# A tuned encoder block: AH preparation, restacking, load order and down-projection sums rearranged

## The chip, the cores and the metric

The kernel runs on one core of a Trainium2 chip as one program. The metric is the device time of one execution in microseconds (us); lower is better. Engines are called as the profile calls them: PE is TensorE (matmuls; PEld its weight loads), DVE is VectorE, ACT is ScalarE, POOL is GpSimd, and SP is SyncE, which here only issues DMAs. An engine runs its instructions strictly in the order in which the program lists them. An instruction that waits holds everything behind it on its engine.

## The reference, cut to what matters

One layer of a bidirectional encoder, all float32, on 1024 rows of 1024 features:

```python
h = rms_norm(x, norm_mix_pre)
z, xbc, dt_raw, u = split(h @ w_in)
y_ssd = ssd_mixer(z, xbc, dt_raw, ...)     # convolution, chunked scan in both directions, gated norm
y_s5  = s5_mixer(u, ...)                   # 64 groups of 16 channels, 64 complex states each
x = x + rms_norm(concat(y_ssd, y_s5) @ w_out, norm_mix_post)
h = rms_norm(x, norm_ffn_pre)
f = (silu(h @ w_gate) * (h @ w_up)) @ w_down          # inner width 2816
return x + rms_norm(f, norm_ffn_post)

# s5_mixer: y = Re(C h) of two linear scans (forward, backward) + d_skip * u
#           g = gelu(y);  return g * sigmoid(g @ glu_w + glu_b)
```

## The kernel before, in words

Matmuls of the large products are done as three products of high and low halves: a cast on ACT makes the high half, a subtraction on DVE the low half.

The stages follow each other in time. First come the norm, the `u` projection and the S5 input. Then the other projection blocks (`blocks`; the last eight make `z`), under which DVE runs the S5 recurrence over the states `SH` (`rec_step`, then `pair_down`). Then the S5 output, 16 batches of four groups each, written out by hand in the loop `for i in range(16)` (`tc.manual_schedule`: the engines get the instructions in the order of the code). Then the GLU, into which a scheduler weaves the SSD units; the output product; the gate and up products of the feed-forward part; the down product; and the tail that norms and stores the result.

S5 output, batch i. `y_mm` (L812 to L814) needs four things: `U`, the batch's input; `W0`, a table of taps read back from DRAM (`w0_load`, L738); `cp`, the powers of the transition (`c_open` on ACT, L697; `c_dir` on DVE, L705 to L707, six instructions a batch); and `AH`, the states of the batch turned into the layout that a matmul wants. `restack` (L802) makes AH with eight copies of 64x254 from SH; the number of them that DVE takes is KN["rsd"], 1 of 8 for b below 11, and none from 11 on; ACT takes the rest. There are two AH tiles, filled in turn, so restack(i+2) has to wait until y_mm(i) has read. The taps of batch i+4 come from `k_mm` (L724, PE) and `k_out` (L730 on ACT, L731 on POOL), are stored to `k_d` from POOL's queue, and `w0_load` reads them back from the same queue. `y_out` (L821, ACT) is the gelu; `g_store` (L825) sends it to DRAM, eight stores for two batches, most from SP's queue. `xt_load` (L683, L685, SP's queue) fetches what c_dir and k_mm start from; in the code it stands behind the stores of its iteration. Before the loop stand restack(0), w0_load(0) and the rest of the preparation.

SSD. `dt_prep` ends with a tile `rhl` (tag "X") that eight DMAs of POOL's queue store to `rr_d` and `na_d` (L894, L895). The tile `X` of the first SSD unit (L904) has the same tag, so its copies wait for these stores.

Down product. Seven products of a Strassen-Winograd scheme, in the order P1, P2, P3, P6, P5, P7, P4, each over 11 values q. One step (a product and a q) is 12 matmuls of 128x512 (L1898). Its operands are prepared by `d_op` some steps ahead: two casts on ACT (L1879) and two subtractions on DVE (L1880). The weights `wd` have four blocks, loaded from SP's queue in P1, P2 and P3. Sums of blocks, which P6, P5, P7 and P4 need, are made by `wd_sums` (L1865) on POOL, four for each q, all of them listed under P3. `half_sum` (L1929, L1933) squares a finished half row and multiplies it by the norm's weight, on POOL except for four at the end. The tail's `final` (L1951) adds the residual, which `final_load` (L1946) fetches.

Of the kernel before, what the change touches and what calls it, by code (L numbers as in the profile page):

```python
# [9 lines left out]
F32 = mybir.dt.float32  # L10
F32R = mybir.dt.float32r
# [7 lines left out]
def _ap(t, off, dims):  # L19
# [49 lines left out]
 'gsp': [],  # L69
 'rsd': 1,  # L70
 'hq': 's',
# [25 lines left out]
 'gB': 7,  # L97
 'rse': 0,
 'ge': 13,
# [33 lines left out]
def hymba_block(ctx, tc, P, out, dbg=None, upto=99):  # L133
# [653 lines left out]
    @pri("rs")  # L787
    def restack(b):

        while len(AHs) < 2:  # L790
            AH = yp.tile([128, 2, 4, 128], F32, name=f"AH{len(AHs)}")
            pool.memset(AH[:, 0, :, 0:1], 0.0)
            pool.memset(AH[:, 1, :, 127:128], 0.0)
            AHs.append(AH)
        AH, p0 = AHs[b % 2], 2 * b
        for d in range(2):
            for j in range(2):
                for comp in range(2):
                    src = SH[64 * j:64 * j + 64, d, (0 if d == 0 else 1):(127 if d == 0 else 128), comp, p0:p0 + 2]
                    dst = AH[64 * comp:64 * comp + 64, d, :, (1 if d == 0 else 0):(128 if d == 0 else 127)]  # L800
                    dst = dst.rearrange("p (q j) k -> p q j k", j=2)[:, :, j, :].rearrange("p q k -> p k q")
                    (dve.tensor_copy if 4 * d + 2 * j + comp >= 8 - KN["rsd" if b < 11 else "rse"] else act.copy)(dst, src)  # L802

    yts = {}

    def y_mm(b):
        U, W0, cp, AH = Us_[b // 2], W0s[b], cps[b], AHs[b % 2]
        c = b % 2
        t = yts[b] = ptmp()
        for g in range(4):  # L810
            o = t[:, 128 * g:128 * g + 128]
            pe.matmul(o, W0[:, 240 * g:240 * g + 128], U[:, 4 * c + g, :], start=True, stop=False)  # L812
            pe.matmul(o, cp[:, 0, g, 1:9, :].rearrange("p n h -> p (n h)"), AH[:, 0, g, :], start=False, stop=False)
            pe.matmul(o, cp[:, 1, g, 0:8, :].rearrange("p n h -> p (n h)"), AH[:, 1, g, :], start=False, stop=True)  # L814
# [14 lines left out]
    def dt_prep():  # L829
# [54 lines left out]
        for d in range(2):  # L884
            pe.matmul(t[:, 128 * d:128 * d + 128], af[:, d].rearrange("p c h -> p (c h)"), (tri_le, tri_ge)[d], start=True, stop=True)
            pe.transpose(t[:, 256 + 128 * d:384 + 128 * d], ln[:, d].rearrange("p c h -> p (c h)"), ident)
        rhl = un.tile([128, 2, 4, 128], F32R, tag="X", name="rhl")
        rh, rl = rhl[:, 0], rhl[:, 1]
        tv = t.rearrange("p (n l) -> p n l", n=4)
# [73 lines left out]
    def unit(q, ssum):  # L963
# [40 lines left out]
        for hf in range(2):  # L1004
# [55 lines left out]
            if hf == 0:  # L1060
                yield
        with hpri("u4"):
            if q % 4 == 0:
                act.activation(ssum, y, AF.Square)
            else:
                sq = io.tile([128, 1024], F32, tag="io", name="sq")
                act.activation(sq, y, AF.Square)
                pd('ss').tensor_tensor(ssum, ssum, sq, op=ADD)
            hl = un.tile([128, 2, 8, 128], F32R, tag="hl", name="hl")
            w = vec2[:, R_N + q:R_N + q + 1]  # L1070
            yv = y.rearrange("p (k l) -> p l k", l=8)
            act.activation(hl[:, 0], yv, AF.Copy, scale=w)
            dve.scalar_tensor_tensor(hl[:, 1], yv, w, hl.bitcast(F32)[:, 0], op0=MUL, op1=SUB)
            Q[KN["cq"]].dma_start(ch_d[128 * q:128 * q + 128], hl.bitcast(F32)[:, 0])
            Q[KN["cq"]].dma_start(cl_d[128 * q:128 * q + 128], hl.bitcast(F32)[:, 1])

    @pri("gn")
    def group_norm(g, ssum):
        t = ptmp()
        sv = ssum.rearrange("p (k l) -> p l k", l=8)  # L1080
        for l in range(8):
            pe.matmul(t[:, l:l + 1], sv[:, l, :], ones[:, 0:1], start=True, stop=True)
        rms_scale(t[:, 0:8], rg[:, g, :], 1.0 / 512, 1e-5)
# [254 lines left out]
    with tc.manual_schedule():  # L1338
        next(cvs)
        pair_powers()  # L1340
        for n, blk in enumerate(blocks):
# [10 lines left out]
            if 0 <= b < 4:  # L1352
# [3 lines left out]
                c_dir(b, 1)  # L1356
            if 0 < b < 4:
                k_batch(b - 1)
            if 0 <= b + 1 < 5 and n < NB - 1:
                xt_load(b + 1)  # L1360
        if KC == 4:
            xt_load(4)
        next(cvs, None)
    rst.close()
# [24 lines left out]

    with tc.manual_schedule():  # L1390
        restack(0)
        w0_load(0)
        w0_load(1)
        u_load(0)
        k_mm(3)
        k_out(3)
        xt_load(5)
        c_open(4)
# [4 lines left out]
        u_load(2)  # L1403
        restack(1)
        qs, oth = [], others()
        for i in range(16):
            y_mm(i)
            if i + 4 < 16:
# [15 lines left out]
            qs = qs[4:]  # L1424
            if i + 6 < 16:
                xt_load(i + 6)
            if i % 2:
# [420 lines left out]
    def wd_load(n, q):  # L1848
# [3 lines left out]
        elif n == "P2":  # L1852
            bl = ((2, 1, 0),)
        elif n == "P3":
            bl = ((3, 1, 1), (1, 0, 1))
        else:
            return
# [3 lines left out]
    def wd_sums(n, q):  # L1861
        w = wd[q]
        l = {"P3": ((0, 1, 0), (1, 3, 1), (3, 3, 0), (2, 2, 3))}.get(n, ())
        for o, a, b in l:
            pool.tensor_tensor(w[:, o], w[:, a], w[:, b], op=SUB)  # L1865

# [60 lines left out]
    def half_sum(l, c):  # L1927
# [3 lines left out]
        if last:  # L1931
            final_scale(l)
        (dve if last else pool).tensor_tensor(f, f, wp2[:, HF[c]], op=MUL)  # L1933

# [76 lines left out]
```

## Time and profile before

| | us |
|---|---|
| three executions | 1672.40, 1672.16, 1668.52; median 1672.16 |
| profiled execution, its own time | 1669.68 |
| its span, first to last instruction | 1667.8 |
| PE busy | 1546.0 (93%) |
| DVE busy | 1241.3 (74%) |
| ACT busy | 730.4 (44%) |
| POOL busy | 461.4 (28%) |
| TensorE clock granted, mean | 0.971 |

Busy time is an average over stages with different limits. By the profile's time slices PE is short of work in the S5 output, about 414 to 522 us, at single places of the GLU, and in the down product between 1520 and 1580 us; between 1060 and 1420 us it hardly pauses.

### The profile page before, as it was taken

The numbers are of one execution on the slowest core, as the hardware profiler recorded it, in microseconds if no ns is written. First come the engines' busy times: TensorE is split into PE (matmuls) and PEld (weight loads), VectorE is DVE, ScalarE is ACT, GpSimd is POOL, SyncE is SP. The second block draws the span as 40 slices with busy tenths as digits, with TensorE's granted clock in tenths as the row PEclk, the third lists the DMA queues.
The fourth block names the chain that finished last, engine by engine and source line by source line (L and its number), as shares of the span: only waits on it lengthen the run. The fifth ranks groups of instructions, "written<-read, shape, count | busy, mean of one in ns | idle before, by whom it ended". The sixth has DMA issues, their size and how long they took to land.

```text
span 1667.8 us, 22199 instructions
## 1 busy us (share of the span) xinstructions
PE 1546.0 (93%) x7980; PEld 1263.7 (76%) x7980; DVE 1241.3 (74%) x1910; ACT 730.4 (44%) x1238; POOL 461.4 (28%) x455
## 2 busy tenths in 40 slices
PE   7999999999777889899999988999999999999897
PEld 6787788777775667778778766788888888787686
DVE  7549998888452687886666578788878887669777
ACT  6345632323887445444343476222223322344352
POOL 2110000000221120111110141555555544249412
PEclk9999999999898989999999998999999999999999
DMA  5553444433877657976588872332222221682234
GB/s 181 149 144 103 127 159 152 133 109 105 207 173 204 189 176 245 289 227 219 189 262 269 291 237 95 122 107 96 95 101 101 95 101 51 242 313 74 92 119 170
DMA packets 250000, 271.58 MB, mean 163 GB/s; under 512 B 29387, under 2 KB 190659, under 8 KB 249891
## 3 DMA queue, kind: packets, MB, share of 16 engines
q1 hardware_dynamic: 224515, 215.96, 41.6%
q0 software_dynamic: 12896, 33.83, 6.4%
q10 hardware_dynamic: 12480, 20.39, 3.4%
q8 instruction: 63, 1.03, 0.3%
q14 instruction: 46, 0.38, 0.1%
HBM read 185.23 MB, written 84.84 MB: 162 GB/s over the span
## 4 chain that ended last, share of the span: by engine, by line
PE 40%; DVE 10%; DMA 8%; issue 4%; ACT 4%; POOL 3%; SPq 0%; DVEq 0%; POOLq 0%; ACTq 0%
PE acc L1592 13%; PE ptmp L1592 10%; PE ptmp L1898 4%; PE acc L1169 3%; PE acc L1898 3%; DVE dop L1880 2%; PE acc L277 2%; DMA m<-m_d 2%; PE ptmp L988 1%; POOL wd L1865 1%; PE ptmp L1054 1%; DMA m_d<-m 1%; DMA oraw<-in_w_out_dram 1%; DVE cacc L756 1%; PE ptmp L1040 1%
## 5 line engine op out<-in xcount | busy, mean ns | idle before, releaser
L1169 PE MATMUL acc<-ohi,cat 128*128 128x512 f32 x512 | 173.3, 404 | 10.8 <-DMA cat<-ch_d 5.7
L277 PE MATMUL acc<-hTh,whi 128*128 128x512 f32 (+1 forms) x456 | 179.5, 394 | 0.4 <-ACT hTh L334 0.4
L277 PE MATMUL acc<-hTl,whi 128*128 128x512 f32 (+1 forms) x456 | 178.7, 392 | 0.5 <-DVE hTl L337 0.5
L277 PE MATMUL acc<-hTh,wlo 128*128 128x512 f32 (+1 forms) x456 | 178.0, 391 | 0.0
L1575 DVE TENSOR_TENSOR wop<-rawp,wop 128x512 fp32r<-128x512 f32 x120 | 137.7, 1148 | 17.9 <-ACT wop L1574 16.7
L1592 PE MATMUL ptmp<-T,wop 128*128 128x512 f32 x528 | 127.8, 398 | 4.1 <-ACT T L1748 3.7
L1592 PE MATMUL acc<-T,wop 128*128 128x512 f32 x528 | 125.7, 393 | 1.7 <-DVE T L1751 1.6
L1898 PE MATMUL ptmp<-dop 128*128 128x512 f32 x528 | 122.0, 392 | 2.9 <-DVE dop L1880 2.9
L1592 PE MATMUL acc<-B,wop 128*128 128x512 f32 x528 | 124.6, 391 | 0.0
L1169 PEld LDWEIGHTS acc<-ohi,cat 128*128 128x128 f32 x512 | 97.7, 192 | 34.4 <-DVE mix L1720 5.4
L1592 PEld LDWEIGHTS ptmp<-T,wop 128*128 128x128 f32 x528 | 101.0, 192 | 27.3 <-ACT T L1748 3.9
L1898 PEld LDWEIGHTS ptmp<-dop 128*128 128x128 f32 x528 | 100.1, 190 | 24.2 <-DVE dop L1880 3.2
L1592 PEld LDWEIGHTS acc<-T,wop 128*128 128x128 f32 x528 | 98.8, 188 | 25.1 <-DVE T L1751 3.4
L1592 PEld LDWEIGHTS acc<-B,wop 128*128 128x128 f32 x528 | 99.0, 188 | 21.9 <-DVE B L1751 0.3
L1607 ACT ACTIVATE cg<-cg 128x512 f32<-128x512 f32 x44 | 27.8, 633 | 183.0 <-DVE cg L1605 183.0
L1574 ACT CAST wop<-rawp 128x512 fp32r<-128x512 f32 x120 | 70.2, 615 | 76.7 <-POOL rawp L1549 51.2
L1880 DVE TENSOR_TENSOR dop<-da,dop 128x512 fp32r<-128x512 f32 x77 | 75.1, 975 | 37.5 <-ACT dop L1879 37.4
L1898 PE MATMUL acc<-dop 128*128 128x512 f32 x396 | 95.6, 398 | 7.4 <-DVE dop L1880 4.7
L1169 PE MATMUL acc<-olo,cat 128*128 128x512 f32 x256 | 101.9, 398 | 0.4 <-DVE olo L1133 0.4
L277 PEld LDWEIGHTS acc<-hTh,whi 128*128 128x128 f32 x456 | 86.7, 190 | 19.4 <-issue 1.7
L277 PEld LDWEIGHTS acc<-hTl,whi 128*128 128x128 f32 x456 | 86.7, 190 | 18.4 <-DVE hTl L337 1.0
L277 PEld LDWEIGHTS acc<-hTh,wlo 128*128 128x128 f32 x456 | 86.7, 190 | 17.1 <-DVE wlo L268 0.2
(368 smaller groups left out, 3400.5 us busy)
## 6 DMA issues: line engine op xcount, KB each, us to landing
ff_d<-cg POOLq DMA_DIRECT2D x77, 256.0 KB, 2.3
da<-ff_d SPq DMA_DIRECT2D x35, 512.0 KB
raw<-in_w_in_dram SPq DMA_DIRECT2D x28, 512.0 KB
cat<-ch_d SPq DMA_DIRECT2D x48, 256.0 KB
cat<-cl_d SPq DMA_DIRECT2D x48, 256.0 KB
wd<-in_w_down_dram SPq DMA_DIRECT2D x44, 256.0 KB
rawp<-in_w_gate_dram SPq DMA_DIRECT2D x10, 1024.0 KB
rawp<-in_w_up_dram SPq DMA_DIRECT2D x10, 1024.0 KB
```

The lines of the kernel that those rows point to most:

```text
L277: pe.matmul(ps, a[:, k, :], b[:, k, sl], start=(k == 0 and n == 0), stop=(k == 7 and n == 2))
L756: (pool if ct in KN['pc'] and k in KN['pk'] else dve).scalar_tensor_tensor(a[:, d], xp[:, r], w[k], a[:, d], op0=MUL, op1=ADD)
L988: pe.matmul(t[:, 256 * s + 128 * d:256 * s + 128 * d + 128], Bt[:, c, g, :], Xw[:, d, c].rearrange("p h e -> p (h e)"), start=True, stop=True)
L1040: pe.matmul(yd[64 * hh:64 * hh + 64, 128 * j:128 * j + 128], X[:, c, 64 * hh:64 * hh + 64], Ms[hh][:, j, :], start=True, stop=True)
L1054: pe.matmul(yo[:, 128 * j:128 * j + 128], Sn[:, d, st, :], CT[:, g, 128 * c:128 * c + 128], start=True, stop=True)
L1169: pe.matmul(ps, c[:, a, k % 4, :], b[:, k % 2, :], start=(k == 0 and n == 0), stop=(k == n_ - 1 and n == 2))
L1574: act.copy(t[:, 0], src)
L1575: dve.tensor_tensor(t[:, 1], src, t.bitcast(F32)[:, 0], op=SUB)
L1592: pe.matmul(ps, a[:, ai, k, :], b[:, bi, k, :], start=(k == 0 and q == 0), stop=(k == 3 and q == 2))
L1607: act.activation(cg[:, 0], cg[:, 0], AF.Silu)
L1880: dve.tensor_tensor(t[:, k, 1], src, t.bitcast(F32)[:, k, 0], op=SUB)
L1898: pe.matmul(ps, t[:, 0, a, 128 * j:128 * j + 128], t[:, 1, b, :], start=(q == 0 and n == 0), stop=(q == NP - 1 and n == 2))
```

## The change

It has five parts.

1. **AH tiles and restacking.** Batches 0 and 1 get AH tiles of their own, in the pool `ck` under the tags "xpad" and "cacc"; batches 2 and 3 start the pair that is then used in turn. From batch 2 on, copies 1, 4 and 7 of the eight run on DVE and five on ACT, up to the last batch; batches 0 and 1 run all eight on ACT. restack(0) moves into the block loop, behind block n = NB-3 (three from the end); restack(1), w0_load(0), w0_load(1) and u_load(0) stand directly behind the last block; k_batch(3) and xt_load(5) move into the block loop.
2. **Table loads.** xt_load(i+6) stands at the head of iteration i, in front of the stores of that iteration.
3. **rhl** takes a buffer of tag "hl" in place of "X".
4. **ssum** (the SSD's gated norm) keeps its elements in another order, so that the matmul reads contiguous columns.
5. **Down.** Block (1,0,1) of wd is loaded under P2 in place of P3. The 44 sums go from POOL to DVE, one for each q under P2, two under P3, one under P6. The 12 multiplications of half_sum that POOL had go to DVE.

The removed entry of the table of settings shifts line numbers: up to line 786 a line of the kernel before is one lower in the new one.

The diff without the table of settings (there 'rsd' becomes (1, 4, 7), and 'rse' goes):

```diff
@@ -787,24 +786,25 @@
     @pri("rs")
     def restack(b):
 
-        while len(AHs) < 2:
-            AH = yp.tile([128, 2, 4, 128], F32, name=f"AH{len(AHs)}")
+        if b < 4:
+
+            AH = (ck if b < 2 else yp).tile([128, 2, 4, 128], F32, name=f"AH{b}", tag=("xpad", "cacc", "AH0", "AH1")[b])
             pool.memset(AH[:, 0, :, 0:1], 0.0)
             pool.memset(AH[:, 1, :, 127:128], 0.0)
             AHs.append(AH)
-        AH, p0 = AHs[b % 2], 2 * b
+        AH, p0 = AHs[b if b < 2 else 2 + b % 2], 2 * b
         for d in range(2):
             for j in range(2):
                 for comp in range(2):
                     src = SH[64 * j:64 * j + 64, d, (0 if d == 0 else 1):(127 if d == 0 else 128), comp, p0:p0 + 2]
                     dst = AH[64 * comp:64 * comp + 64, d, :, (1 if d == 0 else 0):(128 if d == 0 else 127)]
                     dst = dst.rearrange("p (q j) k -> p q j k", j=2)[:, :, j, :].rearrange("p q k -> p k q")
-                    (dve.tensor_copy if 4 * d + 2 * j + comp >= 8 - KN["rsd" if b < 11 else "rse"] else act.copy)(dst, src)
+                    (dve.tensor_copy if 1 < b and 4 * d + 2 * j + comp in KN["rsd"] else act.copy)(dst, src)
 
     yts = {}
 
     def y_mm(b):
-        U, W0, cp, AH = Us_[b // 2], W0s[b], cps[b], AHs[b % 2]
+        U, W0, cp, AH = Us_[b // 2], W0s[b], cps[b], AHs[b if b < 2 else 2 + b % 2]
         c = b % 2
         t = yts[b] = ptmp()
         for g in range(4):
@@ -884,8 +884,8 @@
         for d in range(2):
             pe.matmul(t[:, 128 * d:128 * d + 128], af[:, d].rearrange("p c h -> p (c h)"), (tri_le, tri_ge)[d], start=True, stop=True)
             pe.transpose(t[:, 256 + 128 * d:384 + 128 * d], ln[:, d].rearrange("p c h -> p (c h)"), ident)
-        rhl = un.tile([128, 2, 4, 128], F32R, tag="X", name="rhl")
-        rh, rl = rhl[:, 0], rhl[:, 1]
+        rhl = un.tile([128, 2, 8, 128], F32R, tag="hl", name="rhl")
+        rh, rl = rhl[:, 0, 0:4], rhl[:, 1, 0:4]
         tv = t.rearrange("p (n l) -> p n l", n=4)
         act.copy(rh, tv)
         dve.tensor_tensor(rl, tv, rh.bitcast(F32), op=SUB)
@@ -1060,15 +1060,16 @@
             if hf == 0:
                 yield
         with hpri("u4"):
+
+            yv = y.rearrange("p (k l) -> p l k", l=8)
             if q % 4 == 0:
-                act.activation(ssum, y, AF.Square)
+                act.activation(ssum.rearrange("p (l k) -> p l k", l=8), yv, AF.Square)
             else:
                 sq = io.tile([128, 1024], F32, tag="io", name="sq")
-                act.activation(sq, y, AF.Square)
+                act.activation(sq.rearrange("p (l k) -> p l k", l=8), yv, AF.Square)
                 pd('ss').tensor_tensor(ssum, ssum, sq, op=ADD)
             hl = un.tile([128, 2, 8, 128], F32R, tag="hl", name="hl")
             w = vec2[:, R_N + q:R_N + q + 1]
-            yv = y.rearrange("p (k l) -> p l k", l=8)
             act.activation(hl[:, 0], yv, AF.Copy, scale=w)
             dve.scalar_tensor_tensor(hl[:, 1], yv, w, hl.bitcast(F32)[:, 0], op0=MUL, op1=SUB)
             Q[KN["cq"]].dma_start(ch_d[128 * q:128 * q + 128], hl.bitcast(F32)[:, 0])
@@ -1077,7 +1078,7 @@
     @pri("gn")
     def group_norm(g, ssum):
         t = ptmp()
-        sv = ssum.rearrange("p (k l) -> p l k", l=8)
+        sv = ssum.rearrange("p (l k) -> p l k", l=8)
         for l in range(8):
             pe.matmul(t[:, l:l + 1], sv[:, l, :], ones[:, 0:1], start=True, stop=True)
         rms_scale(t[:, 0:8], rg[:, g, :], 1.0 / 512, 1e-5)
@@ -1354,13 +1355,17 @@
                 c_dir(b, 0)
                 run_steps(KN["r3"])
                 c_dir(b, 1)
-            if 0 < b < 4:
+            if 0 < b < 5:
                 k_batch(b - 1)
-            if 0 <= b + 1 < 5 and n < NB - 1:
+            if 0 <= b + 1 < 6:
                 xt_load(b + 1)
-        if KC == 4:
-            xt_load(4)
-        next(cvs, None)
+            if n == NB - 3:
+                next(cvs, None)
+                restack(0)
+        restack(1)
+        w0_load(0)
+        w0_load(1)
+        u_load(0)
     rst.close()
     hst[0].close()
     hst[1].close()
@@ -1388,22 +1393,16 @@
         yield from ssd_prep(1)
 
     with tc.manual_schedule():
-        restack(0)
-        w0_load(0)
-        w0_load(1)
-        u_load(0)
-        k_mm(3)
-        k_out(3)
-        xt_load(5)
         c_open(4)
         c_dir(4, 0)
         c_dir(4, 1)
         w0_load(2)
         u_load(1)
         u_load(2)
-        restack(1)
         qs, oth = [], others()
         for i in range(16):
+            if i + 6 < 16:
+                xt_load(i + 6)
             y_mm(i)
             if i + 4 < 16:
                 k_mm(i + 4)
@@ -1422,8 +1421,6 @@
             for B, l in qs[:4]:
                 g_store(B, l, Q[KN["gs" if B < KN["gB"] else "gt"][l]])
             qs = qs[4:]
-            if i + 6 < 16:
-                xt_load(i + 6)
             if i % 2:
                 qs += [(i // 2, l) for l in range(8)]
             if i % 2 == 0 and 0 < i and i // 2 + 2 < 8:
@@ -1850,9 +1847,9 @@
             wd.append(fp.tile([128, 4, 512], F32, tag="w8", name="wd", bufs=W_))
             bl = ((0, 0, 0),)
         elif n == "P2":
-            bl = ((2, 1, 0),)
+            bl = ((2, 1, 0), (1, 0, 1))
         elif n == "P3":
-            bl = ((3, 1, 1), (1, 0, 1))
+            bl = ((3, 1, 1),)
         else:
             return
         for b, s_, c in bl:
@@ -1860,9 +1857,9 @@
 
     def wd_sums(n, q):
         w = wd[q]
-        l = {"P3": ((0, 1, 0), (1, 3, 1), (3, 3, 0), (2, 2, 3))}.get(n, ())
+        l = {"P2": ((0, 1, 0),), "P3": ((1, 3, 1), (3, 3, 0)), "P6": ((2, 2, 3),)}.get(n, ())
         for o, a, b in l:
-            pool.tensor_tensor(w[:, o], w[:, a], w[:, b], op=SUB)
+            dve.tensor_tensor(w[:, o], w[:, a], w[:, b], op=SUB)
 
     def d_op(i):
         if i >= len(dprods) or i in dops:
@@ -1930,7 +1927,7 @@
         last = (l, c) in ((4, 0), (5, 0), (6, 0), (7, 0))
         if last:
             final_scale(l)
-        (dve if last else pool).tensor_tensor(f, f, wp2[:, HF[c]], op=MUL)
+        dve.tensor_tensor(f, f, wp2[:, HF[c]], op=MUL)
 
     def final_scale(l):
         dve.tensor_tensor(s5[:, 2, l:l + 1], s5[:, 0, l:l + 1], s5[:, 1, l:l + 1], op=ADD)
```

What the change makes of the order on three engines follows.

ACT at the end of the projection. `zt` is the z block's output, `whi` the next block's high half, `lg` the taps of a batch, AH the restacked states. Before:

```order
L267 CAST whi<-raw 128x1024
L604 ACTIVATE zt<-acc 128x512 x2
L605 DMA z_d<-zt 128x1024
L604 ACTIVATE zt<-acc 128x512
L802 COPY AH_3824<-SH 64x127x2 x7
L604 ACTIVATE zt<-acc 128x512
L605 DMA z_d<-zt 128x1024
L730 COPY lg<-ptmp 128x240
```

Now:

```order
L729 COPY lg<-ptmp 128x240
L802 COPY AH_3700<-SH 64x127x2 x8
L266 CAST whi<-raw 128x1024
L603 ACTIVATE zt<-acc 128x512 x2
L604 DMA z_d<-zt 128x1024
L603 ACTIVATE zt<-acc 128x512
L696 COPY cp<-xtc 128x2x4x16 x2
L603 ACTIVATE zt<-acc 128x512
L604 DMA z_d<-zt 128x1024
L802 COPY AH_3833<-SH 64x127x2 x8
```

The eight copies of batch 0 now stand ahead of the cast of the last block's weights, and those of batch 1 directly behind the last block.

POOL at the same place. `W` is the table W0 of a batch, `edge` a small constant. Before:

```order
L792 MEMSET AH_3824 128x4
L793 MEMSET AH_3824 128x4
L792 MEMSET AH_3827 128x4
L793 MEMSET AH_3827 128x4
L738 DMA W_3838<-k_d 128x1x848
L738 DMA W_3840<-k_d 128x1x848
L1376 MEMSET edge_3814 128x8
```

Now:

```order
L731 DMA k_d<-lg 4x32x240
L792 MEMSET AH_3700 128x4
L793 MEMSET AH_3700 128x4
L792 MEMSET AH_3833 128x4
L793 MEMSET AH_3833 128x4
L737 DMA W_3844<-k_d 128x1x848
L737 DMA W_3846<-k_d 128x1x848
L737 DMA W_3883<-k_d 128x1x848
```

The taps of batch 3 are stored before the memsets, and the loads of W still stand behind the memset of the second AH tile, which now has the buffer of tag "cacc" (the scratch tile of pair_down).

DVE and POOL in the down product, when the operands of P3 are made. `dop` is an operand's low half, `wp` the norm's weight, `fa` the result. Before, these stand on POOL, and DVE has only the two dop rows a step and the results of finished products:

```order
L1865 TENSOR_TENSOR wd<-wd 128x512 x24
L1933 TENSOR_TENSOR fa<-fa,wp_11882 128x512
L1865 TENSOR_TENSOR wd<-wd 128x512 x4
L1933 TENSOR_TENSOR fa<-fa,wp_11882 128x512
L1865 TENSOR_TENSOR wd<-wd 128x512 x4
```

Now, on DVE:

```order
L1901 TENSOR_TENSOR fa<-fa,acc 128x512 x4
L1877 TENSOR_TENSOR dop<-da,dop 128x512
L1877 TENSOR_TENSOR dop<-wd,dop 128x512
L1862 TENSOR_TENSOR wd<-wd 128x512 x2
L1930 TENSOR_TENSOR fa<-fa,wp_11888 128x512
L1877 TENSOR_TENSOR dop<-da,dop 128x512
L1877 TENSOR_TENSOR dop<-wd,dop 128x512
L1862 TENSOR_TENSOR wd<-wd 128x512 x2
```

Each step's two dop subtractions are followed by two sums and, in four steps, by one multiplication; POOL has neither kind of row any more.

## Rows read from the trace of the kernel before

**Rows 1.** Time windows, a stage each: busy us (instructions) by engine, clock, DMA share, GB/s.

```profile
414.00:522.00 108.00, 82.17 (x747) 76.38 (x746) 49.22 (x78) 94.30 (x166) 23.51 (x41) 0.87 0.77 192
...
1431.00:1658.00 227.00, 216.27 (x924) 174.46 (x923) 177.19 (x211) 98.65 (x190) 98.84 (x68) 0.98 0.49 174
```

**Rows 2.** Timeline of PE in the down product: start, us, operation, idle before and releaser.

```profile
1525.59 3.01 PE L1898 MATMUL acc<-dop 128*128 128x512 f32 x12 [0.23 <-DVE dop L1880]
...
1567.64 12.65 PE L1898 MATMUL ptmp<-dop 128*128 128x512 f32 x55
...
1579.68 18.07 PE L1898 MATMUL ptmp<-dop 128*128 128x512 f32 x79
```

**Rows 3.** Timeline of DVE and POOL in the down product.

```profile
1530.57 1.77 DVE L1880 TENSOR_TENSOR dop<-wd,dop 128x512 fp32r<-128x512 f32 x1
...
1533.45 6.83 POOL L1865 TENSOR_TENSOR wd<-wd 128x512 f32<-128x512 f32 x4
...
1572.10 0.68 DVE L1880 TENSOR_TENSOR dop<-da,dop 128x512 fp32r<-128x512 f32 x1
1572.70 0.68 DVE L1880 TENSOR_TENSOR dop<-wd,dop 128x512 fp32r<-128x512 f32 x1
```

**Rows 4.** One group by line, 1420 to 1668 us: count, busy us, mean ns, idle.

```profile
L1865 POOL TENSOR_TENSOR wd<-wd 128x512 f32<-128x512 f32 x44 | 70.5, 1606 | 49.4 <-DMA wd<-in_w_down_dram 35.4 <-DVE dop L1880 11.5
```

**Rows 5.** Time window while the blocks of wd are loaded; columns as in rows 1.

```profile
1460.00:1480.00 20.00, 20.00 (x90) 16.57 (x89) 11.26 (x15) 10.80 (x20) 3.00 (x2) 1.00 1.05 387
```

**Rows 6.** Timeline of the tail's start.

```profile
1640.92 6.03 POOL L1933 TENSOR_TENSOR fa<-fa,wp 128x512 f32<-128x512 f32 x4
1641.06 3.48 DVE L1951 SCALAR_TENSOR_TENSOR fa<-fa,s,xr 128x512 f32<-128x512 f32 x2
...
1650.52 1.42 DVE L1951 SCALAR_TENSOR_TENSOR fa<-fa,s,xr 128x512 f32<-128x512 f32 x2 [2.77 <-DMA xr<-x_d]
```

**Rows 7.** Groups by line of ACT and DVE in the S5 output, 414 to 522 us.

```profile
L802 ACT COPY AH<-SH 64x254 f32<-64x254 f32 x111 | 70.6, 636 | 2.4
...
L730 ACT COPY lg<-ptmp 128x240 f32<-128x240 f32 x13 | 4.6, 356 | 7.3 <-issue 6.5 <-PE ptmp L724 0.8
L697 ACT COPY cp<-xtc 128x128 f32<-128x128 f32 x12 | 3.6, 297 | 2.9 <-DMA xtc<-x_d 2.7
...
L705 DVE TENSOR_TENSOR cp<-xtc,arR 128x512 f32<-128x512 f32 x22 | 15.2, 693 | 18.0 <-DMA xtc<-x_d 17.8
...
L802 DVE COPY AH<-SH 64x254 f32<-64x254 f32 x9 | 3.8, 425 | 11.5 <-PE ptmp L814 11.4
```

**Rows 8.** One line, the gelu of the 16 batches: ns, first and last start.

```profile
L821 ACT ACTIVATE G<-ptmp x16: 590/601/605, 427.5 to 522.2; 128x512 f32<-128x512 f32 x16
```

**Rows 9.** DMA issues of the S5 output: count, KB each, us to landing.

```profile
W<-k_d POOLq DMA_DIRECT2D x16, 424.0 KB, 7.4
...
k_d<-lg POOLq DMA_DIRECT2D x13, 120.0 KB, 5.3
```

**Rows 10.** Timeline around the first S5 batch.

```profile
404.54 1.21 DVE L653 TENSOR_TENSOR SH<-SH,dn 128x1008 f32<-128x1008 f32 x1
...
408.92 0.10 POOL L792 MEMSET AH<- 128x4 f32 x1 [25.74 <-PE acc L277]
...
409.43 1.21 POOL L738 DMA_DIRECT2D W<-k_d  x2 [0.32 <-DVE AH L802]
...
419.91 0.77 PE L812 MATMUL ptmp<-Uy,W 128*128 128x128 f32 x2 [4.29 <-issue]
```

**Rows 11.** Timeline of POOL's DMAs and a DVE copy in the S5 output.

```profile
471.68 0.52 DVE L802 COPY AH<-SH 64x254 f32<-64x254 f32 x1
...
472.01 0.59 POOL L738 DMA_DIRECT2D W<-k_d  x1
```

**Rows 12.** Timeline at the start of the SSD units.

```profile
584.60 1.07 ACT L904 COPY X<-ptmp 128x512 f32<-128x512 f32 x2 [10.83 <-DMA na_d<-rhl]
...
587.08 1.19 PE L988 MATMUL ptmp<-Xw,Bt 128*128 128x128 f32 x4 [9.14 <-DVE Xw L975]
```

More of the change, by code (lines that the diff above doesn't have):

```diff
@@ L69 @@
  'gsp': [],
- 'rsd': 1,
+ 'rsd': (1, 4, 7),
  'hq': 's',
@@ L97 @@
  'gB': 7,
- 'rse': 0,
  'ge': 13,
```

## The prediction

> **What bounds the kernel now.** I read the time windows by stage first, to find where PE is not full. The down product holds PE busy for 216 of 227 us, the S5 output for only 82 of 108 us, where ACT is busy 94 us and the DMA engines 0.77 [rows 1]. So gains can lie only in stretches in which PE starves; the question at each is who ends the wait.
>
> In the down product the timeline of PE shows one such stretch: the eleven steps of P6, from 1525.59 to 1567.64 us, 42.05 us for 132 matmuls, each step started late by "DVE dop" [rows 2]. Where nothing waits, 79 matmuls take 18.07 us, 0.2287 us each [rows 2]; 132 would take 30.2 us. PE loses 11.9 us there. Why DVE is late is in its own timeline: a dop takes 1.77 us while POOL's sums run and 0.68 us, started every 0.60, when POOL is quiet [rows 3]. Two at 1.77 us overlap a little and still need more than the 2.75 us of a step. POOL's 44 sums last 70.5 us [rows 4], longer than the 60 us of two products, so POOL disturbs DVE up to the end of P6.
>
> In the S5 output I read the groups by line. The gelu starts 16 times from 427.5 to 522.2 us, so a batch takes 94.7/15 = 6.31 us [rows 8]. ACT has for each batch seven or eight AH copies of 0.636, mean 7.3 counting DVE's share up to batch 11, and one gelu of 0.60, one lg of 0.36, one cp of 0.30: 4.6 + 1.26 = 5.9 us [rows 7, 8]. ACT all but sets the pace. DVE has six cp instructions of 0.69 and less than one copy, 4.5 us, and it waits 17.8 us in all for the loads of xtc [rows 7].
>
> **The change part by part.**
>
> *Down, sums and multiplications to DVE.* POOL loses all 56 large instructions. What remains of POOL there is small. I take the dop at the cadence of 0.60 us that a quiet POOL gives [rows 3]. DVE's load in its fullest product, P3: 22 dops, 22 sums, 4 results, 4 multiplications, 52 x 0.60 = 31.2 us against PE's 30.2. That is 1.0 us too much, and at 0.68 each it is 5.2 us; operands are made five steps ahead, 5 x 2.75 = 13.7 us, which covers either. The products after it have 37 instructions at most, 22 us. So the stall of 11.9 us should go: -11.9, with bounds -12 and -6 (5.2 of it not hidden). What is late next in that stretch is nothing that I can find; PE paces. The block of wd that is loaded a product earlier adds 11 x 0.256 = 2.8 MB to P2, which then needs two blocks, 5.6 MB, and 2.9 MB of da in 30.2 us, 280 GB/s. The stretch moved 387 GB/s [rows 5], so the load is covered; uncovered, a sum under P2 would wait on it with the dops of the following steps behind it.
>
> *Tail.* The pair of final instructions at 1641.06 took 3.48 us with POOL's four multiplications beside it, and 1.42 us without [rows 6]. The store behind it is issued earlier, and so are the loads of xr that DVE then waits 2.77 us for [rows 6]. The rest of the tail is a serial chain of DVE, ACT and POOL, so 3.48 - 1.42 = 2.06 us come off: -2, bounds 0 and -2.8 (that whole wait). The four multiplications added to DVE fall in time in which it waits.
>
> *S5, pace.* From batch 2 on ACT has 5 x 0.636 + 1.26 = 4.4 us, DVE 6 x 0.69 + 3 x 0.425 = 5.4 us [rows 7]. DVE becomes the busiest of the two, at 0.9 us a batch below today's pace: 15 x 0.89 = 13.4 us. It only comes if DVE no longer waits for xtc, which part 2 is for: the loads go ahead of three or four stores of SP's queue. The stores come later for it; they are wanted only by the GLU's load at the end. The same bytes in less time raise the DMA share from 0.77 to about 0.77 x 108/94 = 0.88, which still fits.
>
> *S5, start.* Here the change costs. y_mm(0) began at 419.91, 10.5 us after the loads of W were issued at 409.43, behind memsets that waited until 408.92 [rows 10]. Now the eight copies of AH(0), 8 x 0.636 = 5.1 us on ACT, stand ahead of the last block's cast, and DVE's low half and its last pair_downs stand behind that cast. The last pair_down ended at 405.75 [rows 10]; I expect it near 411.5. The second AH uses the scratch tile of pair_down, so its memset waits for that, and the loads of W stand behind the memset in POOL's queue: W is issued about 2.4 us later, and so is y_mm(0). Bounds 0 and +5.1. The copies of batches 0 and 1 themselves leave the stage, which the 2.4 hides.
>
> S5 together: -13.4 + 2.4 = -11; I take -10, since stores and loads share the DMA engines. Bounds +3 (no better pace, the late start) and -18 (DVE hidden too, ACT's 4.4 us setting most of the pace).
>
> Here a rule speaks against the change. A DVE copy ran from 471.68 to 472.20 across the start of a POOL issue of W, which took 0.59 us [rows 11]; two issues without a copy took 1.21, 0.60 each [rows 10]. The copy did not hold it up. The Trainium skill, page "SBUF — State Buffer", section "SBUF: two separate sides", says that a float32 copy of VectorE inside SBUF can lock GpSimd out of the port by which it writes the descriptors of its own DMAs. By that rule the three copies a batch, 1.3 us, could delay both of a batch's POOL transfers. The trace disagrees for this copy, and it decides.
>
> *rhl in another buffer.* The copies of X waited 10.83 us for its stores, and PE stood idle 9.14 us before the first state matmul [rows 12]. X is now free earlier. But the next matmuls want what those same stores write, through loads, and a multiplication on POOL, 3.2 us at 1.6 us per 512 columns [rows 4], now precedes some of the stores. I take -4, near the middle; bounds +3.2 and -9.1.
>
> *ssum's order*: as many elements by as many instructions, off the path; nothing.
>
> Sum: -11.9 - 2 - 10 - 4 = -27.9 us. The profiled execution took 1669.68 us, its span 1667.8; so 1641.8 by its own clock. The median of the three runs is 2.5 us above it: 1672.16 - 27.9 = 1644.3, which I give as 1644.
>
> **The rivals.**
>
> *Only the down product and the tail gain.* For it: S5's pace hangs on 12.7 us of transfers a batch, k_d 5.3 and W 7.4 [rows 9], and on DMA engines already 0.77 busy; SSD's wait may pass from X to the loads. The rule on the copies would end here too: two transfers delayed by 1.3 us each, over the four batches that a table is made ahead, cost 0.65 a batch, 10 us, the gain taken. Against it: ACT is busy 94 of 108 us [rows 1]. Time 1672.2 - 13.9 = 1658.
>
> *S5 and SSD give all they can.* ACT's relief sets the pace: -18, SSD -7: 1672.2 - 38.9 = 1633. Against it: DVE's 5.4 us.
>
> *POOL is not what slows DVE* (the change does not do what it says). Then the dops stay at 1.77 us, DVE gets 56 more, and the stall of P6 stays. For it: the casts of ACT wait there too. Against it: 0.68 us as soon as POOL's rows end [rows 3]. Time 1672.2 - 16 = 1656, if the added instructions cost nothing.
>
> *Slower: the S5 output turns into a loop of transfers.* Place: DVE's three copies of batch i+2 wait until y_mm(i) has read the AH; behind them stand the cp instructions of batch i+5, then k_mm, lg, the store of k_d, the load of W, and y_mm(i+5). From rows: 1.3 + 2.1 + 2 + 5.3 + 7.4, about 18 us for five batches. It decides from 5 x 6.31 = 31.5 us on; to bring the kernel 5 us above today, S5 has to lose 17.9 + 5 = 23 us, 1.5 a batch, a loop of 39 us. Then about 1677 or more. For it: nine copies already waited 11.5 us for y_mm [rows 7], and the first W took 10.5 us. Against it: the transfers would have to take 34 us in place of 12.7.
>
> **How the numbers follow.** My forecast 0.57; only down and tail 0.19; all of it 0.12; POOL innocent 0.06; slower loop 0.06. Holding 8 in 10 takes 1631 to 1660: below lie part of the "all" case, above the loop and a part of the others. A change of 0.3%, 5 us, is about what a measurement can tell: faster by more 0.90, within it 0.05, slower by more 0.05.
>
> **What would show it.** In the changed profile: P6 at 2.75 us a step, dops near 0.68 us throughout and no POOL rows of 1.6 us beside them; final pairs of 1.4 us; gelus about 5.4 us apart, ACT no longer busy nine tenths of S5, no waits for xtc; y_mm(0) about 2 us later than 419.9; X copied before na_d is stored. I am wrong if P6 still waits for DVE, if DVE waits for loads in P2, if the gelus stay 6.3 us apart, or if y_mm(0) slips by more than 5 us.

## The result, and the profile after

The changed kernel took 1651.3 us, median of four runs (1649.0 to 1652.9), beside 1670.3 for the kernel before, median of four (1666.6 to 1672.4). The medians are 19.0 us apart. The measured ratio is 0.9876, 95% interval 0.9846 to 0.9907: 1.24% or 20.7 us faster, and the text goes by it. The forecast was a gain of 27.9 us, to 1644. The profiled execution took 1652.8 us, its span 1651.1.

To see where the time came from, I set each PE instruction of one profile beside the same instruction of the other and took the difference of their starts, changed kernel minus kernel before. A negative number is a lead of the changed kernel; it grows where time is gained.

| place (time in the kernel before) | difference of the starts, us |
|---|---|
| 380, before anything that the change touches | +2.5 |
| 420, first S5 batch | +4.8 |
| 560, GLU | -4.3 |
| 587, first SSD state matmuls | -15.9 |
| 640 | -5.3 |
| 1020 to 1420, feed-forward | -4.1 |
| 1440 to 1500, down, before P6 | -2.6 |
| 1580, after P6 | -15.4 |
| end of the span | -16.7 |

The first line is a warning. Up to 380 us both programs do the same, yet one profile is 2.5 us later there. In the other profiles of this study it is between -1.3 and +4.2. A single profile's total cannot be read closer than that; differences between two places can, though the S5 output scatters by 8 us with the same code.

Time windows of the changed kernel, for the S5 output and the down product (columns as in [rows 1]):

```profile
414.00:520.00 106.00, 81.20 (x746) 74.30 (x744) 67.17 (x118) 74.97 (x132) 23.46 (x47) 0.90 0.89 213
1431.00:1641.00 210.00, 210.00 (x918) 173.59 (x917) 158.08 (x262) 98.43 (x188) 6.23 (x8) 0.99 0.52 184
```

In the down product PE is busy throughout. In S5 the load moved from ACT (94 to 75 us) to DVE (49 to 67), and the DMA share rose from 0.77 to 0.89. Neither engine is now full there.

P6 in the timeline of PE, which answers to [rows 2], and DVE while P3 runs, which answers to [rows 3]:

```profile
1522.37 30.08 PE L1895 MATMUL acc<-dop 128*128 128x512 f32 x132
...
1515.84 0.69 DVE L1877 TENSOR_TENSOR dop<-da,dop 128x512 fp32r<-128x512 f32 x1
1516.44 0.69 DVE L1877 TENSOR_TENSOR dop<-wd,dop 128x512 fp32r<-128x512 f32 x1
1517.04 0.69 DVE L1862 TENSOR_TENSOR wd<-wd 128x512 f32<-128x512 f32 x1
```

All 132 matmuls of P6 stand in one row without a wait, 30.1 us in place of 42.05. A dop and a sum start 0.60 us apart, as forecast. The tail's pair of final instructions:

```profile
1625.68 1.41 DVE L1948 SCALAR_TENSOR_TENSOR fa<-fa,s,xr 128x512 f32<-128x512 f32 x2
...
1633.81 1.42 DVE L1948 SCALAR_TENSOR_TENSOR fa<-fa,s,xr 128x512 f32<-128x512 f32 x2 [1.93 <-DMA xr<-x_d]
```

1.41 us in place of 3.48 [rows 6], and the wait for xr is 1.9 us where it was 2.8.

The start of S5 and the gelus, which answer to [rows 10] and [rows 8]:

```profile
412.92 1.21 DVE L652 TENSOR_TENSOR SH<-SH,dn 128x1008 f32<-128x1008 f32 x1
414.19 0.10 POOL L792 MEMSET AH<- 128x4 f32 x1 [15.97 <-DVE SH L652]
414.71 1.22 POOL L737 DMA_DIRECT2D W<-k_d  x2 [0.38 <-issue]
424.71 0.77 PE L812 MATMUL ptmp<-Uy,W 128*128 128x128 f32 x2 [6.39 <-issue]
```

```profile
L821 ACT ACTIVATE G<-ptmp x16: 589/601/619, 432.8 to 518.5; 128x512 f32<-128x512 f32 x16
```

The memset waits for the last pair_down, and W is issued behind it. y_mm(0) comes at 424.7, 4.8 us later than before, 2.3 of it beyond the 2.5 that were there already. The gelus are 85.7/15 = 5.71 us apart, before 6.31.

The waits of the S5 output (engine, line and tile waited for: us, times, longest):

```profile
DVE cp L704 <- DMA xtc<-x_d: 14.3, 5, 5.7
...
PE ptmp L812 <- DMA W<-k_d: 6.1, 2, 5.3
```

DVE still waits 14.3 us for xtc, before 17.8 [rows 7], and PE waits 6.1 us for W, most of it at the last batch.

### The profile page after: what moved, and what is told of

It is laid out like the page before. It is cut to its first block, busy times and chain, and to the rows that moved or that the text cites. A ratio compares the mean times of both kernels' runs of the same rounds, so it can differ in the third digit from the quotient of the medians.

```text
span 1651.1 us, 22178 instructions
## 1 busy us (share of the span) xinstructions
PE 1532.9 (93%) x7980; PEld 1256.0 (76%) x7980; DVE 1240.3 (75%) x1997; ACT 719.5 (44%) x1207; POOL 372.1 (23%) x403
## 4 chain that ended last, share of the span: by engine, by line
PE 64%; DVE 11%; DMA 11%; ACT 6%; issue 5%; POOL 1%; SPq 1%; ACTq 0%; DVEq 0%; POOLq 0%
PE acc L276 17%; PE acc L1589 13%; PE ptmp L1589 10%; PE ptmp L1895 6%; PE acc L1895 5%; PE acc L1170 4%; DMA m<-m_d 2%; DMA m_d<-m 1%; DMA W<-k_d 1%; PE ptmp L557 1%; PE ptmp L1054 1%; PE ptmp L988 1%; DVE cacc L755 1%; PE ptmp L723 1%; DMA cl_d<-ghl 1%
## 5 line engine op out<-in xcount | busy, mean ns | idle before, releaser
L1572 DVE TENSOR_TENSOR wop<-rawp,wop 128x512 fp32r<-128x512 f32 x120 | 137.5, 1147 | 17.9 <-ACT wop L1571 16.7
L1876 ACT CAST dop<-da 128x512 fp32r<-128x512 f32 x77 | 48.0, 623 | 99.5 <-PE acc L1895 38.8
L1610 POOL TENSOR_TENSOR cg<-cg 128x512 f32<-128x512 f32 x44 | 61.8, 1404 | 130.8 <-DVE cg L1605 130.2
```

The source lines that it names most:

```text
L1572: dve.tensor_tensor(t[:, 1], src, t.bitcast(F32)[:, 0], op=SUB)
L1610: pool.tensor_tensor(dst, a, b, op=op)
L1876: act.copy(t[:, k, 0], src)
```

## The experiments

Each ratio is against runs of the kernel before on the same chip. There were three chips, on which the kernel before had medians of 1674.4, 1675.9 and 1675.5 us. A place in a profile is given, where the text says so, with that profile's offset at 380 us taken off.

**e1, the down part alone**, put into the kernel before; with it the 12 multiplications and the block loaded under P2, whose lines are left out here.

```diff
...
-        l = {"P3": ((0, 1, 0), (1, 3, 1), (3, 3, 0), (2, 2, 3))}.get(n, ())
+        l = {"P2": ((0, 1, 0),), "P3": ((1, 3, 1), (3, 3, 0)), "P6": ((2, 2, 3),)}.get(n, ())
-            pool.tensor_tensor(w[:, o], w[:, a], w[:, b], op=SUB)
+            dve.tensor_tensor(w[:, o], w[:, a], w[:, b], op=SUB)
```

> The kernel before with part 5 alone (sums and multiplications on DVE, block (1,0,1) loaded under P2). Theory: POOL's sums were what slowed DVE; P6 runs at 2.75 us a step, the stretch gains about 12.8 us as in the changed kernel, the tail 1 to 2, and the whole comes to -13 to -15 us. Rival, POOL is not the cause or the loads under P2 hold DVE: the dops stay above 1 us and the gain is 0 to -5.

Measured: 1662.2 us, 0.9931 (0.9909 to 0.9953), -11.6 us. P6, from its PE timeline:

```profile
1534.96 30.08 PE L1898 MATMUL acc<-dop 128*128 128x512 f32 x132
```

Between 1500 and 1580 us it gains 12.8 us, in the changed kernel 12.8 as well. The whole gain is a little under the 13 to 15 expected, which its interval (7.9 to 15.2) reaches. So part 5 is what ends P6's stall. But the kernel before has two waits there, and the forecast named one. Its PE and ACT in P6, and ACT's waits from 1500 to 1580 us:

```profile
1529.00 3.02 PE L1898 MATMUL acc<-dop 128*128 128x512 f32 x12 [0.39 <-DVE dop L1880]
1532.39 3.06 PE L1898 MATMUL acc<-dop 128*128 128x512 f32 x12 [0.38 <-DVE dop L1880]
...
1555.60 0.62 ACT L1879 CAST dop<-wd 128x512 fp32r<-128x512 f32 x1 [7.36 <-POOL wd L1865]
...
1556.27 0.51 PE L1898 MATMUL acc<-dop 128*128 128x512 f32 x1 [0.71 <-ACT dop L1879]
...
1561.68 0.62 ACT L1879 CAST dop<-wd 128x512 fp32r<-128x512 f32 x1 [4.95 <-POOL wd L1865]
...
1562.35 0.50 PE L1898 MATMUL acc<-dop 128*128 128x512 f32 x1 [2.05 <-ACT dop L1879]
...
ACT dop L1879 <- POOL wd L1865: 22.4, 4, 7.4
```

Eight steps begin 3.40 us apart, behind a slow dop. The last three take 14.9 us, because ACT's casts wait for the sums themselves, which P6's operands need. At 3.40 each they would take 10.2. So by this estimate some 4.7 of the 11.9 us come of a wait for data, and the rest of slow dops. (In the 4.7 are 1.4 us of slower matmuls: the last eleven took 4.21 us at a granted clock of 0.62, behind the longest wait, and eleven two steps earlier 2.79 at 1.00.) The next three experiments take the two apart.

**e6, POOL additions that nobody waits for**, in the changed kernel.

```diff
+        if n in ("P6", "P5", "P7"):
+            for _ in range(1):
+                pool.tensor_tensor(dmy[:, 0], dmy[:, 0], dmy[:, 1], op=ADD)
...
+    dmy = fp.tile([128, 2, 512], F32, name="dmy")
+    pool.memset(dmy, 0.0)
```

> The changed kernel with 33 additions of 128x512 on POOL in the down product, which read and write a tile that nothing else uses, so nobody waits for them; they run as soon as POOL has finished the gate and up products, from about 1420 us. Theory, POOL slows DVE by running beside it: while they run each addition takes about 1.6 to 1.7 us and each dop about 1.7 in place of 0.68, PE stalls on dop in P1 or P2, +3 to +15 us against the changed kernel. Rival, the stall of before came from waiting for the sums: dops stay at 0.7 us and the time is that of the changed kernel.

Measured: 1662.0 us in its one run. The timeline while the additions run:

```profile
1449.18 13.50 POOL L1865 TENSOR_TENSOR dmy<-dmy 128x512 f32<-128x512 f32 x8
...
1451.28 1.77 DVE L1880 TENSOR_TENSOR dop<-da,dop 128x512 fp32r<-128x512 f32 x1
...
1451.41 3.01 PE L1900 MATMUL ptmp<-dop 128*128 128x512 f32 x12 [0.37 <-DVE dop L1880]
...
1454.80 3.06 PE L1900 MATMUL ptmp<-dop 128*128 128x512 f32 x12 [0.38 <-DVE dop L1880]
...
1476.79 2.99 PE L1900 MATMUL acc<-dop 128*128 128x512 f32 x12 [0.78 <-DVE dop L1880]
1481.85 3.01 PE L1900 MATMUL acc<-dop 128*128 128x512 f32 x12 [2.07 <-DVE dop L1880]
```

The group by line of all 33:

```profile
L1865 POOL TENSOR_TENSOR dmy<-dmy 128x512 f32<-128x512 f32 x33 | 53.1, 1608 | 2.6
```

The 1.77 us and the 3.39 us from step to step are those of P6 before ([rows 3] and the steps shown under e1), at another place and without any data passing between the engines. Under P2, where DVE has a sum to make beside the two dops, the steps are 5.06 us apart, three instructions at 1.69. PE loses 15.2 us between 1440 and 1500 against the changed kernel. Running beside each other is enough for a stall; that the kernel before also waited for the sums is not touched by it.

**e7, the same with memsets**, 99 in place of 33 additions.

```diff
-            for _ in range(1):
-                pool.tensor_tensor(dmy[:, 0], dmy[:, 0], dmy[:, 1], op=ADD)
+            for _ in range(3):
+                pool.memset(dmy[:, 0], 0.0)
```

> As e6 with 99 memsets of 128x512 in place of the 33 additions: POOL is as busy, writes the same tile, and reads nothing. Theory, it is POOL's reads that meet DVE's second input: dops stay near 0.68 us, no stall, the time of the changed kernel. Rival, any POOL work beside DVE slows it: dops above 1 us while they run.

Measured: 1659.0 us in its one run. Groups by line in the down product:

```profile
L1880 DVE TENSOR_TENSOR dop<-da,dop 128x512 fp32r<-128x512 f32 x77 | 54.6, 710 | 43.3 <-ACT dop L1879 42.8
...
L1865 POOL MEMSET dmy<- 128x512 f32 x99 | 52.2, 527 | 5.7
```

POOL is as busy, 52 us beside 53, and the dops stay at 0.71 us (the 48 that run beside a memset average 0.69). PE does not stall: against the changed kernel it shifts by 1.3 us at the start of the stage and by nothing from 1440 us on. So it is not POOL's being busy but its reading. The Trainium skill says this on the page "SBUF — State Buffer", section "Who interferes with whom": a VectorE instruction with two inputs in SBUF contends with a GpSimd instruction that reads SBUF, not with one that only writes. Both halves agree here, 1.77 us beside the additions and 0.71 beside the memsets.

**e8, the sums on POOL at the new places**, in the changed kernel.

```diff
-            dve.tensor_tensor(w[:, o], w[:, a], w[:, b], op=SUB)
+            pool.tensor_tensor(w[:, o], w[:, a], w[:, b], op=SUB)
```

> The changed kernel with the 44 sums on POOL again, at the changed kernel's new places (one per q under P2, two under P3, one under P6; the block loaded early), the multiplications on DVE. Theory that the engine counts: dops slow to 1.2 to 1.8 us from P2 on, and most of the stall comes back, +4 to +12 us against the changed kernel. Rival, that the place counts: begun a product earlier, the sums' slowing is covered by the operands made ahead; within 3 us of the changed kernel.

Measured: 1662.5 us, 0.9913 (0.9881 to 0.9944), by the ratios some 6 us above the changed kernel. The dops average 0.99 us, as in the kernel before (1.01), and PE loses 4.5 us between 1500 and 1560 against the changed kernel:

```profile
1533.33 3.04 PE L1895 MATMUL acc<-dop 128*128 128x512 f32 x12 [0.38 <-DVE dop L1877]
1536.73 3.04 PE L1895 MATMUL acc<-dop 128*128 128x512 f32 x12 [0.36 <-DVE dop L1877]
```

Between 1500 and 1580 us it gains 8.3 of the 12.8 us, about two thirds, with the sums still on POOL. ACT's waits for the sums, 22.4 us there in the kernel before, are gone: begun earlier, the sums are ready when P6's casts want them, and operands made ahead cover part of the slow time. The last third comes from the engine. Both theories hold in part. The 12 multiplications are on DVE here too, so the two thirds include what moving them gave.

**e2, rhl alone**, put into the kernel before.

```diff
-        rhl = un.tile([128, 2, 4, 128], F32R, tag="X", name="rhl")
+        rhl = un.tile([128, 2, 8, 128], F32R, tag="hl", name="rhl")
...
```

> The kernel before with part 3 alone (rhl in a buffer of tag hl). Theory: X no longer waits and PE's pause of 9.1 us before the first state matmul shrinks to about 3, but the GLU, which shares this stretch, takes the time back by its own waits before 650 us; the time stays within 2 us. Rival, the forecast's: the gain stays, -4 us; at most -9.

Measured: 1674.0 us, 0.9994 (0.9972 to 1.0016): no change. X is copied 12.9 us earlier, at 571.7, and PE's pause shrinks from 9.1 to 2.8 us. What follows, in POOL's timeline and then in the chain of waits (start, us, what):

```profile
577.30 0.61 POOL L894 DMA_DIRECT2D rr_d<-rhl  x1 [39.09 <-ACT rhl L890]
577.92 1.92 POOL L975 TENSOR_TENSOR Xw<-X,wdt 128x1024 f32<-128x1024 f32 x1
...
583.96 0.80 POOL L895 DMA_DIRECT2D na_d<-rhl  x1
```

```profile
583.96 6.02 DMA na_d<-rhl
590.00 2.09 DMA la<-na_d
595.15 0.63 ACT ghl L1116
596.72 5.72 DMA cl_d<-ghl
...
613.70 6.24 DMA cl_d<-ghl
```

Xw stands between the stores, and la waits for the last of them. Then the chain runs through the GLU, whose tile ghl waits twice for its own store. Measured from 380 us on, PE is 8.7 us ahead of the kernel before at 587 and 0.5 us behind at 643: the pause was real, and what its removal gave is given back within 60 us. That the chain shown is what takes it back is read from this one profile.

**e3, the S5 parts alone**: parts 1 and 2 of the diff, of which these lines stand for the whole.

```diff
-        while len(AHs) < 2:
+        if b < 4:
...
+            if n == NB - 3:
+                next(cvs, None)
+                restack(0)
...
+            if i + 6 < 16:
+                xt_load(i + 6)
             y_mm(i)
```

> The kernel before with parts 1 and 2 alone (AH tiles and restacking, table loads first). Theory: y_mm(0) comes 2 to 3 us later, the gelus run 5.7 us apart in place of 6.3, the last batch waits for its W; S5 ends 6 to 8 us earlier and the whole gains about 6 us. Rival: the end of S5 is hidden behind what the GLU waits for, and the whole gains under 2 us; or the forecast's -10.

Measured: 1662.7 us, 0.9938 (0.9918 to 0.9958), -10.4 us, more than the 6 expected. The gelus run from 433.9 to 522.6, 5.91 us apart; this profile is of the slowest of the six runs, 1669.1 us. The three ratios of e1, e2 and e3 multiply to 0.9931 x 0.9994 x 0.9938 = 0.9863, the changed kernel's 0.9876 within its interval: the parts add. Part 4 has no run of its own, and the product leaves nothing for it.

**e4, the split of the copies alone**, everything else as before.

```diff
-(dve.tensor_copy if 4 * d + 2 * j + comp >= 8 - KN["rsd" if b < 11 else "rse"] else act.copy)(dst, src)
+(dve.tensor_copy if 4 * d + 2 * j + comp in ((1, 4, 7) if b > 1 else (7,)) else act.copy)(dst, src)
```

> The kernel before with the split of the copies alone (from batch 2 on copies 1, 4 and 7 on DVE, five on ACT); AH tiles, start and order of the loads as before. Theory that ACT set the pace: most of the better pace is here without any of the cost at the start, gelus 5.6 to 5.8 us apart, -7 to -10 us. Rival, that the loads of xtc behind the stores set the pace once ACT is relieved: gelus 6.0 to 6.3 us apart, 0 to -4 us.

Measured: 1661.7 us, 0.9924 (0.9899 to 0.9949), -12.7 us, more than the 7 to 10 expected; gelus 427.0 to 510.4, 5.56 us apart. One line of the change carries its whole S5 gain.

**e11, the split with the loads in front.**

```diff
         for i in range(16):
+            if i + 6 < 16:
+                xt_load(i + 6)
             y_mm(i)
...
-            if i + 6 < 16:
-                xt_load(i + 6)
```

> As e4 (the split alone) with the loads of xtc and yk at the head of the iteration in front of the stores; AH tiles and start as before. Theory that the loads in front cost by holding the stores, on whose end the gelu's tile waits: gelus 5.7 to 5.9 us apart, waits of the gelu for its stores of some us, 0 to 4 us slower than e4. Rival, that the loads in front help and the loss in the changed kernel is from its start alone: DVE's waits for xtc under 5 us, as fast as e4 or up to 3 us faster.

Measured: 0.9911 (0.9879 to 0.9944); gelus 5.76 us apart. The waits, among them one that the forecast ruled out:

```profile
ACT G L821 <- DMA g_d<-G: 10.3, 4, 4.1
DVE cp L705 <- DMA xtc<-x_d: 9.8, 6, 4.2
```

DVE waits 9.8 us for xtc, 10.0 in the split alone, so the loads gain nothing; the gelu now waits 10.3 us for stores to free its tile, for which it does not wait in the split alone. In time the two kernels cannot be told apart.

**e5, W ahead of the second AH**, and **e9, the whole start mended**, both in the changed kernel; the last three lines are in e9 alone.

```diff
-        restack(1)
         w0_load(0)
         w0_load(1)
         u_load(0)
+        restack(1)
...
-            next(oth, None)
+            if i > 1:
+                next(oth, None)
```

> The changed kernel with the loads of the first two W tables and of the first U ahead of restack(1), so that they no longer stand behind the memset of the second AH. Theory: W issues when its own buffer is free, about 2 to 3 us earlier, y_mm(0) with it, and 2 us of the 2.4 lost at the start come back; the whole 0 to 3 us faster than the changed kernel. Rival: the buffer of W is freed no earlier than the memset was, or the DMA engines hold it; no change.

> As e5, and the SSD preparation (whose load of BT waits for the buffer of the first AH, with the loads of xtc behind it in SP's queue) begins two batches later. Theory that both holds at the start make what the split loses in the changed kernel: xtc of the eighth batch is issued at once, the wait of 5.7 us for it goes, S5 ends 4 to 6 us earlier than in the changed kernel, -23 to -25 us against before. Rival: the end of S5 is set by the round of k_d and W in the last batches, and no more than 2 us are won.

Measured: 0.9877 (0.9843 to 0.9910) and 0.9852 (0.9811 to 0.9894). W is issued earlier, and y_mm(0) starts 6.5 us earlier than in the changed kernel (415.7 beside 422.2, offsets taken off), more than expected:

```profile
408.81 1.22 POOL L737 DMA_DIRECT2D W<-k_d  x2 [9.29 <-PE acc L276]
...
419.46 0.38 PE L812 MATMUL ptmp<-Uy,W 128*128 128x128 f32 x2
```

(That is e5's profile, 3.8 us late at 380.) But the gelus then run 94.7 and 91.7 us, in place of 85.7, and the last one comes no earlier (518.5 and 515.6 beside 516.0, offsets taken off). The time lost at the start is not what limits the stage. The time of e9, 24.8 us below the kernel before, lies in the 23 to 25 expected, but not for the reason given: DVE's waits for xtc are 15.8 us, the longest 6.0, and its interval holds the changed kernel's ratio.

**e12, no copies** for batches 2 to 15, in the kernel before.

```diff
-        for d in range(2):
+        for d in range(2 if b < 2 else 0):
             for j in range(2):
```

> The kernel before without the AH copies of batches 2 to 15 (its S5 output is then not the reference's): ACT has 1.3 us a batch, DVE 4.1, PE as before. Theory that once the copies are split the round of transfers (k_d stored, W read back) sets the pace: gelus 5.2 to 5.6 us apart, not much under the 5.6 of e4, S5 10 to 14 us shorter than before. Rival, that ACT and DVE still set it in e4: gelus 4.2 to 4.6 us apart, S5 over 25 us shorter.

Measured: 1662.8 us in its one run. Gelus 427.2 to 514.4, 5.81 us apart. Two windows of S5, the stretch from the first gelu to the last, the same stretch of the changed kernel, and then the waits of e12; columns as before:

```profile
460.00:480.00 20.00, 17.43 (x198) 16.15 (x197) 12.60 (x20) 5.27 (x14) 6.42 (x10) 1.00 0.83 184
480.00:500.00 20.00, 15.21 (x147) 14.12 (x146) 10.63 (x17) 3.10 (x9) 6.32 (x11) 0.88 0.91 215
...
427.20:514.40 87.20, 68.41 (x660) 64.17 (x659) 40.43 (x63) 23.27 (x50) 21.24 (x36) 0.92 0.90 217
...
432.80:518.50 85.70, 67.47 (x659) 62.49 (x658) 52.96 (x93) 66.14 (x120) 20.44 (x39) 0.92 0.92 226
```

```profile
DVE cp L705 <- DMA xtc<-x_d: 35.3, 8, 13.1
```

ACT has little left to do, 23 of 87 us, and the stage is no faster than with the split: 5.81 us against 5.56, above the 5.2 to 5.6 expected. So once ACT is relieved, neither ACT nor DVE sets the pace. Nearest their limit are then the transfers: DVE waits 35 us for xtc, and the DMA share is 0.90 here and 0.92 in the changed kernel. PE comes next, busy 68 of 87 us. That transfers set the pace is read from these rows; whether by the amount moved or by the round of k_d and W, no run separates.

**e10, split and down part alone**: the diffs of e4 and e1 together in the kernel before.

> The kernel before with two things alone: the split of the copies of batches 2 to 15 (as in e4) and the down part (as in e1). Theory that the rest of the change (AH tiles under the projection, loads first, rhl) gives nothing or costs: the two gains add, -11.6 and -12.7 us, to about -24 us, 0.985 to 0.987 of before, some 3 to 5 us better than the changed kernel. Rival, that the split was lucky in its run and the rest of the change helps: -17 to -20 us, no better than the changed kernel.

Measured: 1649.6 us, median of five, 0.9844 (0.9818 to 0.9871). These two edits of the kernel before do all that the whole change does; the interval overlaps the changed kernel's 0.9846 to 0.9907, so a gain over it is not shown.

## Why the prediction was right, and where its sizes were off

- **Down, -11.9: right in size, and in cause for the larger part.** 12.8 us in the profile. The cause named, POOL's work beside DVE's subtractions, is shown by e6 and e7. But the reading that each step of P6 began late behind a dop of DVE holds for nine of the eleven steps; two began behind casts of ACT that waited for the sums (shown under e1). The sum took the whole 11.9 us, so it needed no division, and the change removed both waits. The covers held too; P3 on DVE and the block loaded early made PE wait nowhere.
- **Tail, -2: right.** Between the end of P6 and the end of the span five profiles with the down part (the changed kernel, e1, e5, e9, e10) gain 1.3 to 2.5 us; e2, e3, e4 and e11, which lack it, lie between -0.2 and 0.5.
- **S5, start, +2.4: right**, by the steps forecast: 2.3 us in y_mm(0). The last pair_down ended at 414.1, which is 411.7 without the 2.5, and 411.5 was expected.
- **S5, pace, -13.4: reached in part, and by another limit.** Over the five profiles with the new S5 code (the changed kernel, e3, e6, e7 and e8; spans of the gelus 80.7 to 88.7 us, mean 84.7) and the three with the old (the kernel before, e1 and e2; 93.7 to 98.6, mean 95.7) the gain is 11.0 us. The step that failed is "It only comes if DVE no longer waits for xtc, which part 2 is for": those waits went only from 17.8 to 14.3 us, and e12 shows that DVE's 5.4 us is not the limit. The 5.4 us were also taken for all 15 intervals, while [rows 7] has the cp instructions of eleven batches in the stage (22 on L705, two a batch). And the risen DMA share was priced at 1 us, where transfers seem to hold the stage. That three quarters of the term came all the same is luck in part: the pace that stopped it, 5.6 us, lies close to the 5.4 forecast for another reason. With the start, the last gelu came 7.4 us earlier in the mean, where I took -10.
- **"The stores come later for it; they are wanted only by the GLU's load": wrong.** The gelu's tile waits for them, 8.8 us in e3, 10.3 in e11, 1.0 in the changed kernel's profile.
- **SSD, -4: not there.** The first ra-la product did come earlier, 592.3 in e2 against 594.2, some 4.5 us with that profile's 2.6 taken off. The forecast counted it to the end of the program without asking what the GLU, which shares the engines up to 640 us, would wait for next. e2 by itself is -1.0 us with an interval of -4.7 to +2.7.
- **The sum.** 12.8 + 2 + 7.4 + 0 is 22, against 20.7 measured with an interval of 15.5 to 25.7 us. So the 7 us that are missing against the forecast are the SSD term and a quarter of the S5 term.
- **The rivals.** "Only the down product and the tail gain" is refuted by e3 and e4, "POOL is not what slows DVE" by e6. "A loop of transfers" looked to the transfers, where the limit seems to lie, but with the wrong sign: the gain stops at 5.6 us a batch and does not turn into a loss.
- **The copies against POOL's DMAs.** In the changed kernel ten of POOL's 28 issues of k_d and W ran beside a DVE copy. k_d took 0.72 us with and without one; W 0.59 to 0.77 with one, 0.58 to 0.61 without. The rule of the Trainium skill that the prediction weighed against the change (page "SBUF — State Buffer", section "SBUF: two separate sides") cost nothing that can be seen.

Open: the split alone ends S5 at 511.9 us in the mean of two profiles (offset at 380 taken off), the changed kernel's S5 at 515.5 in the mean of five, which scatter from 511.3 to 519.2. Whether the moved start and loads really cost 3 us is not settled.

## What to carry to other kernels

Before work is moved to a second engine because it is idle, look at what the first engine's instructions cost while the second one runs: 0.68 us alone and 1.77 beside it made more than half of the down product's loss here. Then look at when the moved results are wanted: in P6 they came too late. Before a relieved engine's next load is taken as the new pace, try the stage with that work left out: here one run showed that neither of the two engines was the next limit. Follow a removed wait to the place where its time is given back or kept: here 8.7 us were gone 60 us later.

## What was not expected of the hardware

POOL's 33 additions of the experiment took 1.61 us each beside DVE, though nothing depended on them, and the dops beside them 1.77, the same as in the kernel before. Eight additions took 13.50 us, 1.69 each, and the steps of two dops were 3.39 us apart: an instruction of one engine seems to pass after each one of the other. No run shows what such an addition takes while DVE is quiet. Memsets of the same size took 0.53 us and disturbed nothing. And the part of the program that no edit touches moved by up to 5.6 us from profile to profile, and the span of the gelus with the same code by 8 us.
